# Seven quarter products for the queries and keys of three retention heads, and value groups that add up in PSUM

## The chip, the cores and the metric

The kernel runs on one core of one Trainium2 chip. The metric is device time of one execution in microseconds (us). Engines are named as in the profile: PE is TensorE's matmul row, PEld its weight loads (which overlap PE), DVE is VectorE, ACT is ScalarE, POOL is GpSimd, and SP issues most DMAs.

## The reference, cut to what matters

One transformer block on 512 tokens of width 1024, in float32: a stick-breaking attention with 16 heads and a retention with 4 heads side by side, mixed by gates, then a feed-forward layer. The part that matters here, for each retention head of query/key width 256 and value width 512:

```python
hmix = modulate(rmsnorm(x, g_norm1[l]), shift1, scale1)          # 512 x 1024
proj = jnp.einsum('bsd,de->bse', hmix, w_in[l])
sb_q, sb_k, sb_v, r_q, r_k, r_v, r_g, br = jnp.split(proj, IN_SPLITS, axis=-1)
...
rq = rotary(r_q.reshape(b, s_len, RET_HEADS, RET_QK_DIM))
rk = rotary(r_k.reshape(b, s_len, RET_HEADS, RET_QK_DIM)) * (RET_QK_DIM ** -0.5)
rv = r_v.reshape(b, s_len, RET_HEADS, RET_V_DIM)
o_ret = retention(rq.transpose(0, 2, 1, 3), rk.transpose(0, 2, 1, 3), rv.transpose(0, 2, 1, 3))
o_ret = head_rmsnorm(o_ret.transpose(0, 2, 1, 3)).reshape(b, s_len, RET_V_WIDTH)
o_ret = jax.nn.silu(r_g) * o_ret
... jnp.einsum('bse,ed->bsd', o_ret, w_proj_ret[l]) ...
```

The rotary turn takes the first and second 128 of a head's 256 columns as a pair and gives `t1*cos - t2*sin` and `t1*sin + t2*cos`.

## The kernel before

**Precision.** Every float32 operand of a matmul is split in two: ScalarE copies it, rounded, to a high part (`hi`), and VectorE subtracts to get the low part (`lo`). `mm3` then issues three matmuls, high by high, high by low, low by high. `weight(key)` loads 512 KB of weights into a buffer "raw" (three of them) and splits them (lines 206 and 208); `sv_parts` does the same for weights that are loaded already (lines 879 and 883). The split weights lie in four "whi" and four "wlo" buffers, 128 x 1024 each.

**The seven products.** A product of a 2 x 2 block matrix by another can be done with seven block products in place of eight. The kernel does so for the value and gate columns of retention heads 1 to 3 (the groups "vg") and for the stick-breaking values (group "sv"). The activations' block sums S1 to S4 are formed once (`sv_acts`) and stay in SBUF, keyed A11, A12, A22, S1, S2, S3, S4. For each group, `seven` loads the weights' quarters b11, b12, b21, b22, forms their sums on VectorE (`sub`, line 1006), splits them, and calls `sv_product` once for each key: 24 matmuls of 512 columns into two PSUM banks. The feed-forward part does the same with `product`, 24 matmuls of 256 columns into one bank.

**How a group adds up before the change.** P1 (the product A11) is copied from PSUM to SBUF by ScalarE (line 1028), A12 is added to it in PSUM and stored, and the other sums are formed on VectorE from an SBUF tile and a PSUM bank: P1 + S2 (line 1051), + S3 (1056), + A22 (1061); S1 is copied out (1066) and added (1070), S4 goes on in S1's banks and is added last (1073). The order of products is A11, A12, S2, S3, the scores, A22, S1, the outputs, S4. In the last group ("sv") there are no scores and outputs, and A11 comes ahead of the gate and the projection.

**A retention head.** In the loop over `h` the order on TensorE is: `ret_qk(h + 1)`, the queries and keys of the next head by four `gemm`s of 8 x 3 matmuls of 512 columns, with head `h`'s gate (`ret_gate`, 16 transposes, line 787) in between; then `seven`, which runs the projection of head `h` (`ret_proj`, eight gemms of 12 matmuls over the weights "pr") and the value group of head `h + 1` with its scores and outputs. `ret_gate` needs all four products of VectorE at line 783. The rotary turn (lines 699 to 701, then a split into a "q" tile) reads the queries and keys from PSUM.

**Buffers.** PSUM has eight banks: four "ps", three "z", one "av". The SBUF tags that the change touches are "raw" (3) and "araw" (2) for loaded weights, "s" (8 tiles of 128 x 1024), "t" (7 of 128 x 512) and "q" (8).

**Order.** Outside a few blocks, the order of the instructions on each engine is made when the program is built, by a scheduler that follows the order in which they are written but takes a later one where an earlier one is not ready by its own estimate. Each engine then works through its list in that order. DMAs stand in SP's list in the same way, and a load that waits for its buffer holds up the loads behind it.

Of the kernel before, what the change touches and what calls it, by code (L numbers as in the profile page):

```python
# [19 lines left out]
P = 128  # L20
# [23 lines left out]
def weight_plan():  # L44
# [20 lines left out]
    for h in range(RH):  # L65
        for i in range(2):
            add(("rq", h, i), "w_in", 0, 8, rng(C_RQ + h * RK + i * P, P))
        for i in range(2):
            add(("rk", h, i), "w_in", 0, 8, rng(C_RK + h * RK + i * P, P))
        if h == 0:  # L70
            for part in range(4):
                add(("rg", 0, part), "w_in", part * 256, 2, rng(C_RG, 512))
        for i in range(4):
            add(("pr", h, i), "w_proj_ret", h * RV, 4, rng(i * 256, 256))
# [41 lines left out]
def kernel(  # L116
# [567 lines left out]
    def ret_qk(h, banks=None, between=lambda: None):  # L684
        res = []
        for key in ("rq", "rk"):
            if banks:
                p1, p2 = banks.pop(0), banks.pop(0)
            else:
                p1, p2 = ps(), ps()  # L690
                gemm(p1, weight((key, h, 0)), hs)
                if key == "rq" and h > 1:
                    between()
                gemm(p2, weight((key, h, 1)), hs)
                if key == "rq" and h == 1:
                    between()
            for c1, c2, op in ((cosT, sinT, ALU.subtract), (sinT, cosT, ALU.add)):
                m1, m2 = tmp(), tmp()
                nc.vector.tensor_mul(m1, p1, c1)
                nc.vector.tensor_mul(m2, p2, c2)  # L700
                nc.vector.tensor_tensor(m1, m1, m2, op=op)
                hl = pair("q")
                split(hl[:, 0, :], hl[:, 1, :], m1)
                res.append(hl)
        return res
# [302 lines left out]
    def seven(name, h, gate, store, scores=lambda: None, outs=lambda: None, first=False, early=3):  # L1008
# [14 lines left out]
        p1 = [tmp() for _ in PI]  # L1023

        def opening():
            x = sv_product("A11", w1)
            for t, o in zip(p1, x):
                nc.scalar.activation(t, o, AF.Copy)  # L1028
            return x

        if first:
            ahead(0)
            ahead(1)
            x = opening()
# [5 lines left out]
        if not first:  # L1040
            x = opening()
# [5 lines left out]
        w7 = [sv_parts(t) for t in b12]  # L1047
        for two in loaded:
            ada_after(last_low[0], two)
        for t, o in zip(p1, sv_product("S2", w6)):  # L1050
            nc.vector.tensor_add(t, t, o)
        w4 = [sv_parts(t) for t in b21]
        b22 = [sv_raw(name, 1, 1, n, "s") for n in PI]
        u3 = [tmp() for _ in PI]
        for t, u, o in zip(u3, p1, sv_product("S3", w7)):
            nc.vector.tensor_add(t, u, o)
        w5 = [sv_parts(t) for t in b11]
        scores()
        c21 = [tmp() for _ in PI]
        for t, u, o in zip(c21, u3, sv_product("A22", w4)):  # L1060
            nc.vector.tensor_add(t, u, o)
        store(1, 0, c21)
        x = sv_product("S1", w5)
        c22 = [tmp() for _ in PI]
        for t, o in zip(c22, x):
            nc.scalar.activation(t, o, AF.Copy)
        w3 = [sv_parts(t) for t in b22]
        outs()
        for t, u in zip(c22, u3):
            nc.vector.tensor_add(t, t, u)  # L1070
        store(1, 1, c22)
        for t, o in zip(p1, sv_product("S4", w3, x)):
            nc.vector.tensor_add(t, t, o)
        store(0, 1, p1)

    qk = ret_qk(0, qk_ps)
# [8 lines left out]
    for h in range(3):  # L1085
        ys = []
        qk = ret_qk(h + 1, between=lambda: ys.extend(ret_gate(h, *outs, sgs)))
# [790 lines left out]
```

## Time and profile before

| | |
|---|---|
| Time, median of 3 runs | 1110.66 us (1110.65 to 1110.95) |
| Profiled execution, span | 1109.0 us |
| PE busy | 1101.6 us (99%) |
| PEld busy | 940.5 us (85%) |
| DVE busy | 868.6 us (78%) |
| ACT busy | 564.8 us (51%) |
| POOL busy | 43.3 us (4%) |
| DMA | 181.41 MB, mean 164 GB/s |

The profiled execution has no time of its own beside its span; the runs' median stands 1.7 us above that span. Busy time of PE is modelled, since matmuls overlap: a row's duration is longer than the distance to the next row, and the distance is what counts. A line "L229" is the one line in `mm` that issues all matmuls, so matmuls are told apart by their tiles: "ps<-h,whi" writes a "ps" bank, with the moving operand in an "h" tile and the weights in "whi". In the windows view each engine's busy time in a stretch is followed by the number of instructions in brackets.

### The profile page before, as it was taken

The numbers are of one execution on the slowest core, as the hardware profiler recorded it, in microseconds if no ns is written. First come the engines' busy times: TensorE is split into PE (matmuls) and PEld (weight loads), VectorE is DVE, ScalarE is ACT, GpSimd is POOL, SyncE is SP. The second block draws the span as 40 slices with busy tenths as digits, with TensorE's granted clock in tenths as the row PEclk, the third lists the DMA queues.
The fourth block names the chain that finished last, engine by engine and source line by source line (L and its number), as shares of the span: only waits on it lengthen the run. The fifth ranks groups of instructions, "written<-read, shape, count | busy, mean of one in ns | idle before, by whom it ended". The sixth has DMA issues, their size and how long they took to land.

```text
span 1109.0 us, 15098 instructions
## 1 busy us (share of the span) xinstructions
PE 1101.6 (99%) x5635; PEld 940.5 (85%) x5635; DVE 868.6 (78%) x1292; ACT 564.8 (51%) x935; POOL 43.3 (4%) x69
## 2 busy tenths in 40 slices
PE   9999999999999999999999999999999999999997
PEld 7888888888888888888888888889988888888887
DVE  7996967848868759478678876667999988888875
ACT  5454445445444645265565654357745644554445
POOL 0000000010020020000000000000000000000000
PEclk9999999999999999999999999999999999999999
DMA  8733662583486295887676448662443544444112
GB/s 339 295 108 103 215 206 85 172 208 114 155 177 219 78 206 180 225 237 226 187 200 174 144 159 307 241 171 58 130 138 115 151 133 133 131 117 124 67 39 76
DMA packets 59112, 181.41 MB, mean 164 GB/s; under 512 B 7328, under 2 KB 8352, under 8 KB 59040
## 3 DMA queue, kind: packets, MB, share of 16 engines
q1 hardware_dynamic: 53568, 166.82, 45.9%
q0 software_dynamic: 5472, 13.63, 7.8%
q8 instruction: 44, 0.72, 0.3%
q14 instruction: 28, 0.23, 0.1%
HBM read 148.97 MB, written 16.78 MB: 149 GB/s over the span
## 4 chain that ended last, share of the span: by engine, by line
PE 96%; DVE 2%; ACT 1%; issue 0%; DVEq 0%; ACTq 0%
PE ps L229 71%; PE z L229 14%; PE av L229 8%; PE ps L651 1%; PE z L787 0%; PE av L651 0%; ACT q L1234 0%; DVE h L1544 0%; DVE s L1279 0%; DVE h L1279 0%; DVE o L1214 0%; ACT h L1545 0%; PE av L787 0%; ACT t L1708 0%; DVE h L1608 0%
## 5 line engine op out<-in xcount | busy, mean ns | idle before, releaser
L229 PE MATMUL ps<-h,whi 128*128 128x512 f32 (+1 forms) x1026 | 293.2, 372 | 0.0
L229 PEld LDWEIGHTS ps<-h,whi 128*128 128x128 f32 x1026 | 184.1, 189 | 30.9 <-ACT h L440 0.2
L206 ACT ACTIVATE whi<-raw 128x1024 fp32r<-128x1024 f32 (+1 forms) x104 | 108.7, 1045 | 187.6 <-PE ps L229 142.1
L229 PE MATMUL ps<-h,wlo 128*128 128x512 f32 (+1 forms) x513 | 187.9, 370 | 0.0
L208 DVE TENSOR_TENSOR wlo<-raw,whi 128x1024 fp32r<-128x1024 f32 (+1 forms) x104 | 124.7, 1199 | 57.6 <-ACT whi L206 57.0
L229 PEld LDWEIGHTS ps<-h,wlo 128*128 128x128 f32 x513 | 96.7, 188 | 16.5
L229 PE MATMUL ps<-s,whi 128*128 128x512 f32 x320 | 98.9, 390 | 0.0
L229 PE MATMUL ps<-q,whi 128*128 128x512 f32 (+1 forms) x368 | 98.5, 385 | 0.0
L883 DVE TENSOR_TENSOR wlo<-s,whi 128x1024 fp32r<-128x1024 f32 x46 | 56.1, 1220 | 40.4 <-ACT whi L879 40.4
L229 PEld LDWEIGHTS ps<-q,whi 128*128 128x128 f32 x368 | 67.9, 188 | 13.5 <-DVE t L1372 0.2
L879 ACT ACTIVATE whi<-s 128x1024 fp32r<-128x1024 f32 x47 | 49.7, 1057 | 50.2 <-PE ps L229 44.3
L229 PE MATMUL ps<-whi,h 128*128 128x512 f32 x222 | 71.6, 391 | 0.0
L229 PEld LDWEIGHTS ps<-s,whi 128*128 128x128 f32 x320 | 60.1, 188 | 12.7 <-DVE s L208 0.3
L229 PE MATMUL ps<-s,wlo 128*128 128x512 f32 x160 | 62.3, 389 | 0.0
L229 PE MATMUL ps<-q,wlo 128*128 128x256 f32 (+1 forms) x328 | 59.3, 293 | 0.0
L229 PEld LDWEIGHTS ps<-q,wlo 128*128 128x128 f32 x328 | 48.2, 190 | 3.3
L229 PEld LDWEIGHTS ps<-whi,h 128*128 128x128 f32 x222 | 41.7, 188 | 9.5 <-ACT t L1028 0.6
L229 PE MATMUL ps<-wlo,h 128*128 128x512 f32 x111 | 43.3, 390 | 0.0
L229 PE MATMUL ps<-whi,q 128*128 128x512 f32 x128 | 40.7, 389 | 0.0
L641 DVE TENSOR_TENSOR_SCAN s<-s,table 128x1024 f32<-128x1024 f32 x16 | 36.6, 2288 | 4.6 <-ACT s L635 4.5
L229 PE MATMUL z<-q,q 128*128 128x256 f32 (+3 forms) x224 | 40.1, 325 | 0.0
L229 PEld LDWEIGHTS z<-q,q 128*128 128x128 f32 x224 | 34.8, 189 | 3.0 <-DVE q L208 0.2
(364 smaller groups left out, 2200.0 us busy)
## 6 DMA issues: line engine op xcount, KB each, us to landing
raw<-wp SPq DMA_DIRECT2D x136, 512.0 KB, 3.9
araw<-wp SPq DMA_DIRECT2D x30, 512.0 KB, 4.4
s<-wp SPq DMA_DIRECT2D x24, 512.0 KB, 5.2
s<-wada SPq DMA_DIRECT2D x20, 512.0 KB, 7.4
sraw<-wada SPq DMA_DIRECT2D x16, 512.0 KB, 8.5
q<-qp SPq DMA_DIRECT2D x32, 256.0 KB, 4.3
araw<-wada SPq DMA_DIRECT2D x12, 512.0 KB, 4.6
spill<-o POOLq DMA_DIRECT2D x24, 256.0 KB, 4.7
```

What stands on the lines that cost most here:

```text
L206: nc.scalar.activation(dst_hi, src, AF.Copy, scale=scale)
L208: return (eng or nc.vector).tensor_sub(dst_lo, src, f(dst_hi))
L229: return nc.tensor.matmul(o, lhs, rhs, start=start, stop=stop, skip_group_check=True).ins
L641: nc.vector.tensor_tensor_scan(n[:, ::-1], n[:, ::-1], d[:, ::-1], 0.0, op0=ALU.mult, op1=ALU.max)
L651: nc.tensor.transpose(at[bank][:, c : c + P], t[:, a + j * P : a + (j + 1) * P], ident)
L879: nc.scalar.activation(hi, t, AF.Copy)
L883: last_low[0] = nc.vector.tensor_sub(lo, t, f(hi))
```

## The change

The queries and keys of heads 1 to 3 are made by seven products (`quarter_product`, 24 matmuls of 256 columns) from four weight quarters, loaded under the new keys ("qk", h, half, c). The products add up in three PSUM banks: x (A11, then A12), z (a ScalarE copy of A11, then S2, S3, A22), v (S1, then S4). ScalarE copies the results to SBUF tiles `q` and `k` in the order that the rotary turn wants; two VectorE adds complete the keys. The weight sums are formed on VectorE in the loaded buffers. The gate of the head before (`between`) comes after the second product.

The value groups keep their seven products but add up in the same way: x's two banks are copied by ScalarE to two more banks z, S2, S3 and A22 go on in z, with copies out after S2 and S3, and four VectorE adds remain of ten. Their order is now A11, A12, S2, S1, S3, the scores, A22, the outputs, S4.

```diff
--- before.py
+++ after.py
@@ -63,11 +63,11 @@
         add(("sq", p), "w_in", 0, 8, rng(C_Q + p * P, P))
         add(("sk", p), "w_in", 0, 8, rng(C_K + p * P, P))
     for h in range(RH):
-        for i in range(2):
-            add(("rq", h, i), "w_in", 0, 8, rng(C_RQ + h * RK + i * P, P))
-        for i in range(2):
-            add(("rk", h, i), "w_in", 0, 8, rng(C_RK + h * RK + i * P, P))
-        if h == 0:
+        if h:
+            for half in range(2):
+                for c, at in enumerate((C_RQ, C_RK)):
+                    add(("qk", h, half, c), "w_in", half * 512, 4, rng(at + h * RK, RK))
+        else:
             for part in range(4):
                 add(("rg", 0, part), "w_in", part * 256, 2, rng(C_RG, 512))
         for i in range(4):
@@ -681,27 +681,16 @@
 
     head_pe = {}
 
-    def ret_qk(h, banks=None, between=lambda: None):
+    def rotary(p1, p2):
         res = []
-        for key in ("rq", "rk"):
-            if banks:
-                p1, p2 = banks.pop(0), banks.pop(0)
-            else:
-                p1, p2 = ps(), ps()
-                gemm(p1, weight((key, h, 0)), hs)
-                if key == "rq" and h > 1:
-                    between()
-                gemm(p2, weight((key, h, 1)), hs)
-                if key == "rq" and h == 1:
-                    between()
-            for c1, c2, op in ((cosT, sinT, ALU.subtract), (sinT, cosT, ALU.add)):
-                m1, m2 = tmp(), tmp()
-                nc.vector.tensor_mul(m1, p1, c1)
-                nc.vector.tensor_mul(m2, p2, c2)
-                nc.vector.tensor_tensor(m1, m1, m2, op=op)
-                hl = pair("q")
-                split(hl[:, 0, :], hl[:, 1, :], m1)
-                res.append(hl)
+        for c1, c2, op in ((cosT, sinT, ALU.subtract), (sinT, cosT, ALU.add)):
+            m1, m2 = tmp(), tmp()
+            nc.vector.tensor_mul(m1, p1, c1)
+            nc.vector.tensor_mul(m2, p2, c2)
+            nc.vector.tensor_tensor(m1, m1, m2, op=op)
+            hl = pair("q")
+            split(hl[:, 0, :], hl[:, 1, :], m1)
+            res.append(hl)
         return res
 
     def tok_proj_wide(banks, ws):
@@ -1020,60 +1009,110 @@
             elif i == 3:
                 sub(b12, b11, b11)
 
-        p1 = [tmp() for _ in PI]
-
-        def opening():
-            x = sv_product("A11", w1)
-            for t, o in zip(p1, x):
+        def copied(z, us):
+            for t, o in zip(us, z):
                 nc.scalar.activation(t, o, AF.Copy)
-            return x
+            return us
 
         if first:
             ahead(0)
             ahead(1)
-            x = opening()
+            x = sv_product("A11", w1)
         ys = gate()
         ret_proj(h, ys, ahead)
         b21 = [sv_raw(name, 1, 0, n, "raw") for n in PI]
         sub(b22, b12, b12)
         sub(b22, b11, b22)
         if not first:
-            x = opening()
+            x = sv_product("A11", w1)
+        z = copied(x, [ps() for _ in PI])
         w2 = [sv_parts(r) for r in b21]
         loaded = [ada_early("s") for _ in range(early)]
         w6 = [sv_parts(t) for t in b22]
         sub(b21, b22, b21)
         store(0, 0, sv_product("A12", w2, x))
-        w7 = [sv_parts(t) for t in b12]
+        w5 = [sv_parts(t) for t in b11]
         for two in loaded:
             ada_after(last_low[0], two)
-        for t, o in zip(p1, sv_product("S2", w6)):
+        sv_product("S2", w6, z)
+        u2 = copied(z, [tmp() for _ in PI])
+        w7 = [sv_parts(t) for t in b12]
+        v = sv_product("S1", w5)
+        b22 = [sv_raw(name, 1, 1, n, "s") for n in PI]
+        w4 = [sv_parts(t) for t in b21]
+        sv_product("S3", w7, z)
+        c22 = copied(z, [tmp() for _ in PI])
+        scores()
+        for t, o in zip(c22, v):
             nc.vector.tensor_add(t, t, o)
-        w4 = [sv_parts(t) for t in b21]
-        b22 = [sv_raw(name, 1, 1, n, "s") for n in PI]
-        u3 = [tmp() for _ in PI]
-        for t, u, o in zip(u3, p1, sv_product("S3", w7)):
-            nc.vector.tensor_add(t, u, o)
-        w5 = [sv_parts(t) for t in b11]
-        scores()
-        c21 = [tmp() for _ in PI]
-        for t, u, o in zip(c21, u3, sv_product("A22", w4)):
-            nc.vector.tensor_add(t, u, o)
-        store(1, 0, c21)
-        x = sv_product("S1", w5)
-        c22 = [tmp() for _ in PI]
-        for t, o in zip(c22, x):
-            nc.scalar.activation(t, o, AF.Copy)
+        store(1, 1, c22)
         w3 = [sv_parts(t) for t in b22]
+        store(1, 0, sv_product("A22", w4, z))
         outs()
-        for t, u in zip(c22, u3):
-            nc.vector.tensor_add(t, t, u)
-        store(1, 1, c22)
-        for t, o in zip(p1, sv_product("S4", w3, x)):
+        for t, o in zip(u2, sv_product("S4", w3, v)):
             nc.vector.tensor_add(t, t, o)
-        store(0, 1, p1)
-
-    qk = ret_qk(0, qk_ps)
+        store(0, 1, u2)
+
+    def quarter_product(key, w, o, first=False):
+        hi, lo = (tiles(t) for t in w)
+        ah, al = sacts[key]
+        for i in PI:
+            c, oc = slice(i * P, i * P + P), o[:, i * 256 : i * 256 + 256]
+            for k in range(4):
+                mm3(oc, hi[:, k, c], lo[:, k, c], ah[k], al[k],
+                    first and i == 0 and k == 0, i == 1 and k == 3)
+
+    def ret_qk(h, between):
+
+        def load(half, c, tag):
+            r = wpool.tile([P, WCOLS], F32, tag=tag, bufs=BUFS[tag], name=nm(tag))
+            nc.sync.dma_start(r, wp[WIDX["qk", h, half, c]])
+            return r
+
+        def turned(t):
+            return t.rearrange("p (f h c) -> p h f c", f=2, h=2)
+
+        def as_two(o):
+            return o.rearrange("p (f c) -> p f c", f=2)
+
+        b11, b12 = (load(0, c, "araw") for c in PI)
+        b21, b22 = (load(1, c, "raw") for c in PI)
+        w1 = sv_parts(b11)
+        nc.vector.tensor_sub(b11, b12, b11)
+        w5 = sv_parts(b11)
+        nc.vector.tensor_sub(b12, b22, b12)
+        w3 = sv_parts(b22)
+        nc.vector.tensor_sub(b22, b22, b11)
+        x, z, v = ps(), ps(), ps()
+        quarter_product("A11", w1, x, True)
+        nc.scalar.activation(z, x, AF.Copy)
+        quarter_product("S1", w5, v, True)
+        w6 = sv_parts(b22)
+        between()
+        p5 = tmp()
+        nc.scalar.activation(p5, v, AF.Copy)
+        quarter_product("S2", w6, z)
+        w7 = sv_parts(b12)
+        q, k = raw_quarter("s"), raw_quarter("s")
+        kt, qt = turned(k), turned(q)
+        nc.scalar.activation(kt[:, 0], as_two(z), AF.Copy)
+        quarter_product("S4", w3, v)
+        nc.vector.tensor_add(kt[:, 0], kt[:, 0], as_two(v))
+        w2 = sv_parts(b21)
+        nc.vector.tensor_sub(b21, b21, b22)
+        quarter_product("S3", w7, z)
+        nc.scalar.activation(kt[:, 1], as_two(z), AF.Copy)
+        nc.vector.tensor_add(kt[:, 1], kt[:, 1], as_two(p5))
+        w4 = sv_parts(b21)
+        quarter_product("A12", w2, x)
+        nc.scalar.activation(qt[:, 0], as_two(x), AF.Copy)
+        k1, k2 = rotary(k[:, 0:S], k[:, S:])
+        quarter_product("A22", w4, z)
+        nc.scalar.activation(qt[:, 1], as_two(z), AF.Copy)
+        q1, q2 = rotary(q[:, 0:S], q[:, S:])
+        return q1, q2, k1, k2
+
+    qk = rotary(*qk_ps[:2]) + rotary(*qk_ps[2:])
     vt = ret_v(v_ps)
     st = ret_scores(0, qk)
     sgs = ret_silu(0)
@@ -1084,7 +1123,7 @@
     outs = ret_out(0, st, vt)
     for h in range(3):
         ys = []
-        qk = ret_qk(h + 1, between=lambda: ys.extend(ret_gate(h, *outs, sgs)))
+        qk = ret_qk(h + 1, lambda: ys.extend(ret_gate(h, *outs, sgs)))
         st, outs = {}, []
         vt = lambda: [rvts[b] for b in range(4)]
         seven(("vg", h + 1), h, lambda: ys, rv_store, lambda: st.update(ret_scores(h + 1, qk)),
```

## The prediction

> **What bounds the kernel now.** I read the page first: its busy shares and the chain of work that ended last.
>
> ```profile
> span 1109.0 us, 15098 instructions
> PE 1101.6 (99%) x5635; PEld 940.5 (85%) x5635; DVE 868.6 (78%) x1292; ACT 564.8 (51%) x935; POOL 43.3 (4%) x69
> PEclk9999999999999999999999999999999999999999
> PE 96%; DVE 2%; ACT 1%; issue 0%; DVEq 0%; ACTq 0%
> ```
>
> TensorE is on the chain for 96% of the span at an undiminished clock, so a change pays only as it shortens TensorE's row, or costs as it opens gaps in it. Next the busy times by stretch. The last five of the first six rows below are one retention head (92.8 to 187.0); the seventh row is the next head's queries and keys; the last two rows are a pure 512-column stretch and one of the feed-forward part, whose products already have the new form.
>
> ```profile
> core 0: us, PE busy (x) PEld busy (x) DVE busy (x) ACT busy (x) POOL busy (x), PEclk, DMA share, GB/s
> 86.00:92.80 6.80, 6.80 (x32) 5.63 (x31) 2.79 (x4) 5.26 (x13) 0.00 (x0) 1.00 0.01 5
> 92.80:116.30 23.50, 23.50 (x113) 19.71 (x112) 18.97 (x40) 8.87 (x13) 0.00 (x0) 1.00 0.49 169
> 116.30:138.10 21.80, 21.80 (x98) 18.05 (x97) 19.98 (x21) 9.19 (x14) 0.00 (x0) 1.00 0.58 196
> 138.10:159.90 21.80, 21.80 (x97) 17.86 (x96) 11.88 (x18) 9.08 (x11) 0.00 (x0) 1.00 0.70 234
> 159.90:181.60 21.70, 21.70 (x104) 18.16 (x103) 17.60 (x28) 12.50 (x21) 2.55 (x4) 1.00 0.24 89
> 181.60:187.00 5.40, 5.40 (x26) 4.46 (x25) 4.02 (x16) 1.75 (x3) 0.00 (x0) 1.00 0.01 2
> 187.00:210.50 23.50, 23.50 (x113) 19.72 (x112) 19.29 (x26) 10.48 (x14) 0.00 (x0) 1.00 0.51 181
> ...
> 106.50:159.50 53.00, 53.00 (x236) 1.00 0.62 209
> ...
> 785.00:795.00 10.00, 10.00 (x85) 10.00 (x85) 9.86 (x13) 5.99 (x9) 0.00 (x0) 1.00 0.34 76
> ```
>
> TensorE is busy for the whole of every row: the retention heads have no gap that the change could close. VectorE is second: 18.97 + 19.98 + 11.88 + 17.60 + 4.02 = 72.5 of 94.2 us in the head, fullest just where the change adds to it (116.3 to 138.1: 92%), with some 10 us free behind that. The clock is 1.00 throughout.
>
> **TensorE's saving.** Queries and keys of heads 1 to 3 are now four gemms of 8 x 3 matmuls of 512 columns, 96 a head. They become seven products of 2 x 4 x 3 = 24 matmuls of 256 columns, 168 a head. The prices are in TensorE's timeline: 24 of 512 columns, and 24 of 256 in the same order of hi and lo, each read to the start of the next row.
>
> ```profile
> 138.07 5.60 PE L229 MATMUL ps<-v,h 128*128 128x512 f32 x24
> 143.51 0.39 PE L229 MATMUL ps<-whi,q 128*128 128x512 f32 x1
> ...
> 781.95 3.04 PE L229 MATMUL z<-q,h 128*128 128x256 f32 x24
> 784.83 3.04 PE L229 MATMUL ps<-v,s 128*128 128x256 f32 x24
> ```
>
> (143.51 - 138.07) / 24 = 0.2267 us and (784.83 - 781.95) / 24 = 0.120 us. So 96 x 0.2267 = 21.76 becomes 168 x 0.120 = 20.16: 1.60 us a head, 4.80 us for three. An eighth of the columns goes, but a 256-column matmul costs 6.7 ns more than half a 512-column one, which takes 1.1 of the 2.7 us. The weight-load column says why: 10.00 of 10.00 us at 785 against about 18 of 21.8 in the 512-column rows, so there the loads set the pace.
>
> [...]
>
> **New waits on PSUM.** The value groups keep x (two banks) and now copy it by ScalarE to z (two more of the four "ps" banks); A12 goes on in x; S2, S3 and A22 add into z in turn. Before, S2 had fresh banks and one of its matmuls slipped in (143.51) while the copies ran. Now S2 needs the copy too and S1 finds no bank, so A12's first matmul waits. The old last group shows that wait uncovered: S1 ends, its banks are copied (L1066), S4 goes on in them.
>
> ```profile
> 431.15 1.28 ACT L1066 ACTIVATE t<-ps 128x512 f32<-128x512 f32 x2 [0.93 <-PE ps L229]
> 431.18 0.39 PE L229 MATMUL ps<-wlo,q 128*128 128x512 f32 x1
> 431.41 0.39 PE L229 MATMUL ps<-whi,q 128*128 128x512 f32 x1
> ...
> 431.81 0.50 PE L229 MATMUL ps<-whi,o 128*128 128x512 f32 x1
> ```
>
> 431.81 - 431.41 - 0.227 = 0.17 us. It comes three times (A11 to A12; in the last group x is ready a whole projection earlier) and once in the last group from S3 to A22, which in the heads has the scores between; the old S1-to-S4 wait goes. Net 3 x 0.17 = 0.51 us. Bounds: 0 (filled, as at 143.51) to 4 x 1.28 = 5.1 (both copies bare); I take the row of the same wait. The other reuses have a product or the scores between: S2 to S3 has S1, S1 to S4 has A22 and the outputs. S1 still takes x's banks only after the store of A12, as S3 did. A22 now directly precedes the outputs (S1 stood there): their first nine matmuls need only the older value blocks, 9 x 0.227 = 2.0 us against one 0.6 split and one 0.68 subtraction, and S4 can be put in; 0.
>
> **VectorE and ScalarE.** The prices, from the groups by line (VectorE's counted from 60 to 440 us, ScalarE's over the whole run):
>
> ```profile
> L883 DVE TENSOR_TENSOR wlo<-raw,whi 128x1024 fp32r<-128x1024 f32 x16 | 19.3, 1220 | 10.2 <-ACT whi L879 10.2
> L208 DVE TENSOR_TENSOR q<-t,q 128x512 fp32r<-128x512 f32 x16 | 10.9, 682 | 0.4 <-ACT q L206 0.4
> L1006 DVE TENSOR_TENSOR s<-s,s 128x1024 f32<-128x1024 f32 x8 | 9.5, 1216 | 0.0
> L1051 DVE TENSOR_TENSOR t<-t,ps 128x512 f32<-128x512 f32 x8 | 5.4, 680 | 0.0
> L1070 DVE TENSOR_TENSOR t<-t,t 128x512 f32<-128x512 f32 x8 | 5.3, 688 | 0.3 <-ACT t L1066 0.3
> ...
> L879 ACT ACTIVATE whi<-raw 128x1024 fp32r<-128x1024 f32 x19 | 20.2, 1061 | 29.6 <-PE ps L229 26.7 <-DVE mod L265 1.6 <-PE av L229 1.3
> ...
> L1028 ACT ACTIVATE t<-ps 128x512 f32<-128x512 f32 x8 | 4.8, 598 | 11.7 <-PE ps L229 11.4
> ```
>
> Each head's queries and keys gain three low parts and four weight sums (7 x 1.22 = 8.5) and two adds (1.4): +9.9 us of VectorE. Each value group loses six of its ten adds (L1051, L1056, L1061, L1070, L1073, two each): 6 x 0.68 = -4.1. Net +5.8 us a head: 78.3 of 92.8 us, 84%; on the whole it fits. ScalarE gains three high parts (3.2), six copies (3.6) and two in the group (1.2): +8 us on 41 of the head's 94; hidden.
>
> Where it is tight is the queries' and keys' stretch, 20.2 + 2.0 (transposes) = 22.2 us from A11's start (t = 0). The four whi/wlo buffers let the low parts for A11 and S1 be made behind the old A22, during the outputs and S4, where VectorE is least loaded. From t = 0: last adds 1.4, S4's part, the sum, S2's part 3.7, four gate parts 2.7, S3's part 1.2, adds and sums 2.6, parts for A12 and A22 2.4: 14 us for 22.2, before any rotation. Buffer by buffer: S2's part is made by about 4 and needed at 7.8; S3's by 6, at 13.5; A12's by 9, at 16.4; A22's by 13, at 19.3. Leads of 4 to 7 us. The rotations (16 x 0.68 = 10.9) move behind, into the projection's first 10 us, and push the group's weight sums into the idle third behind 138. In the 785 stretch VectorE is 9.86 of 10 us busy and TensorE has no gap. Bounds for late weights: 0, to what rival B gives; I allow 0.17 us, the shortest wait shown, for each product group of a head: 0.51.
>
> **Queues.** A head's four loads stay 512 KB each on SP's queue; two move from "raw" to "araw" buffers. SP's later loads queue behind them: in head 1 the two modulation loads wait for the second "araw" release at about t = 6; in the later value loads b22 waits for the "s" buffers of the unrotated q and k, free at about t = 30, needed by t = 44.
>
> ```profile
> raw<-wp SPq DMA_DIRECT2D x136, 512.0 KB, 3.9
> araw<-wp SPq DMA_DIRECT2D x30, 512.0 KB, 4.4
> ```
>
> At 4 us a load both are hidden; if not, 4.4 us once. POOL's queue is untouched. The gate's transposes come 5.8 us into the stretch (10.9 before in head 1, 5.4 in 2 and 3). Head 1's four gate products then end just in time, head 2's earlier:
>
> ```profile
> 98.34 0.74 DVE L783 SCALAR_TENSOR_TENSOR t<-av,sm,t 128x512 f32<-128x512 f32 x1
> ...
> 189.92 1.40 DVE L783 SCALAR_TENSOR_TENSOR t<-z,sm,t 128x512 f32<-128x512 f32 x2
> ```
>
> Head 1: 98.34 + 0.74 = 99.1 against 92.8 + 5.8 = 98.6; 0.5 us late, covered by S2, whose weights are ready from the idle 86 to 92.8. Head 2: 4.3 us behind the start at 187.0; in time.
>
> **Sum.** -4.80 + 0.51 + 0.51 = -3.78 us on the profiled span of 1109.0: 1105.2. The median of the runs, 1110.66, stands 1.7 above that span; I keep that difference: **1106.9 us**. A difference under 0.2% (2.2 us: 1108.4 to 1112.9) counts as no change.
>
> **Rivals.** *B, slower: the projection's first weights stand behind the rotation.* Both are VectorE's, and the rotation is written earlier. If q's rotation (8 x 0.68 = 5.4, beginning a copy of 0.6 after A22) is served first, TensorE waits 0.6 + 5.4 + 1.2 = 7.2 us in each head; half of it in front gives 3.6, so -3.8 + 10.8: **1117.7**. It cancels the gain from 1.3 us a head and is slower from 2.0. For: VectorE is 92% busy in that stretch. Against: the weights' input is ready seven us before q is, and today the two kinds alternate without a gap. *C, no change: bank reuse in the quarter products.* Five reuses a head (A11-S2, S2-S3, S1-S4, A11-A12, S3-A22); at 0.17 each 15 x 0.17 = 2.6: **1109.5**. Against: a product of 2.9 us stands between, and copy and add take 1.3. *D, slower: the last group's z is taken while the last projection runs.* x already holds two of the four banks; with one left each of eight gemms shows its copy, 8 x (0.59 + 0.17) = 6.1: **1113.0**. For: x is complete long before; against: z's copies are written behind the projection. *E: the 256-column matmul runs at half the 512-column price,* 0.1133: 2.7 us a head, 1103.5 after the same waits. [...]
>
> **How the numbers follow.** Forecast 0.64, with its own range 1105.0 to 1108.4 (no wait at all gives 1110.7 - 4.8 = 1105.9; another 0.9 is a quarter of the way from there to E); B 0.12, C 0.17, D 0.05, E 0.02. Faster 0.66, same 0.17, slower 0.17. The range 1105.0 to 1112.0 takes in the forecast and C and leaves out B, D and E, 0.19.
>
> **What would show it.** TensorE's row: seven runs of 24 256-column matmuls per head, 2.88 us each; head to head 1.4 us shorter; a pitch of about 0.4 us once at A12. VectorE nearly full from A11 to the end of the projection, idle time behind it shrunk. Wrong would make it: gaps of over 1 us before S2, A22 or the first projection matmul (B), or a projection of the last head longer than 22 us (D).

## The result, and the profile after

The changed kernel takes **1112.22 us** (median; 1111.07 to 1114.87), the kernel before 1110.66 us (1110.25 to 1111.1) beside it: a ratio of 1.0018, interval 1.0011 to 1.0024. The forecast was 1106.9 us in a range of 1105.0 to 1112.0, and faster. The kernel is 1.6 us slower instead. Its 17 runs also spread four times as far, 3.8 us against 0.9.

The page of the profile after: span, busy times, chain of work that ended last.

```profile
span 1110.2 us, 15580 instructions
PE 1098.1 (99%) x5851; PEld 945.5 (85%) x5851; DVE 882.8 (80%) x1295; ACT 585.4 (53%) x970; POOL 40.8 (4%) x69
PE 88%; DVE 7%; ACT 2%; DMA 1%; issue 1%; SPq 0%; DVEq 0%; ACTq 0%
```

TensorE is busy for 3.5 us less, and the span is 1.2 us longer. Its share of the chain fell from 96 to 88%, VectorE's rose from 2 to 7%: TensorE now waits for VectorE. Where, says the waits view of the changed kernel for TensorE's matmuls, 88 to 500 us (who waited for whom: total us, times, longest; for the kernel before, this view is empty for that stretch):

```profile
PE ps L229 <- DVE wlo L208: 1.5, 1, 1.5
PE z L776 <- DVE t L772: 1.3, 1, 1.3
PE ps L229 <- DVE s L208: 0.6, 1, 0.6
PE ps L229 <- DVE wlo L872: 0.5, 1, 0.5
```

A stretch is named here after the head whose queries and keys open it; the gate and the projection in it work on the outputs of the head before. The first wait is in head 1's projection (from 127.7 us: 1.69 us between two matmuls beyond the usual distance), the second at the first transpose of head 1's gate (95.0: 1.50), the third at the last projection, in the last group (382.9: 0.81), the fourth at S3 of head 1's value group (163.3: 0.70). From head to head (the starts of A11's first matmul at 92.26, 189.12, 282.20 and 375.27, the last of them the last group's, and the first stick-breaking turn at 483.41) the lengths are 96.86, 93.08, 93.07 and 108.14 us, against 94.21, 94.08, 94.09 and 107.03 before: +2.65, -1.00, -1.02, +1.11. So the gain is there in heads 2 and 3, and head 1 and the last group take back more than it.

Busy time by stretch after: queries and keys and projection of head 1, the same of head 2, and head 3's projection; then head 3's projection before.

```profile
92.30:115.70 23.40, 22.06 (x185) 21.86 (x184) 20.26 (x39) 11.43 (x17) 0.00 (x0) 1.00 0.41 139
115.70:139.30 23.60, 22.08 (x98) 17.95 (x97) 22.33 (x27) 12.33 (x18) 0.00 (x0) 1.00 0.77 255
...
189.10:211.00 21.90, 21.90 (x185) 21.88 (x184) 18.97 (x24) 13.26 (x19) 0.00 (x0) 1.00 0.41 128
211.00:233.20 22.20, 22.12 (x98) 17.96 (x97) 22.20 (x26) 12.33 (x19) 6.12 (x7) 1.00 0.96 231
...
304.10:326.30 22.20, 22.09 (x99) 17.95 (x98) 22.20 (x26) 12.25 (x19) 5.97 (x7) 1.00 0.98 234
```

```profile
304.60:326.40 21.80, 21.80 (x98) 18.05 (x97) 16.94 (x18) 9.19 (x14) 5.96 (x7) 1.00 0.75 144
```

The last two rows are the ones that matter. During head 3's projection VectorE was busy for 16.94 of 21.80 us before and is busy for 22.20 of 22.20 us after; the DMA engines went from 0.75 to 0.98. In head 1's projection VectorE has 22.33 of 23.60. That TensorE waits where VectorE's list puts something else in front of what it needs is what the experiments below test.

The saving itself, from TensorE's timeline of head 2: the starts of A11's and S1's first two matmuls.

```profile
189.12 0.40 PE L229 MATMUL ps<-h,whi 128*128 128x256 f32 x2
...
191.99 0.40 PE L229 MATMUL ps<-q,whi 128*128 128x256 f32 x2
```

(191.99 - 189.12) / 24 = 0.1196 us a matmul, as forecast.

### The profile page after: what moved, and what is told of

Read it like the earlier page. It is cut to its first block, busy times and chain, and to the rows that moved or that the text cites. A ratio compares the mean times of both kernels' runs of the same rounds, so it can differ in the third digit from the quotient of the medians.

```text
span 1110.2 us, 15580 instructions
## 1 busy us (share of the span) xinstructions
PE 1098.1 (99%) x5851; PEld 945.5 (85%) x5851; DVE 882.8 (80%) x1295; ACT 585.4 (53%) x970; POOL 40.8 (4%) x69
## 2 busy tenths in 40 slices
DMA packets 59115, 181.45 MB, mean 163 GB/s; under 512 B 7328, under 2 KB 8352, under 8 KB 59040
## 4 chain that ended last, share of the span: by engine, by line
PE 88%; DVE 7%; ACT 2%; DMA 1%; issue 1%; SPq 0%; DVEq 0%; ACTq 0%
PE ps L229 64%; PE z L229 14%; PE av L229 8%; PE ps L651 1%; DVE wlo L208 1%; DVE t L690 1%; DVE wlo L872 1%; DVE t L689 1%; DVE s L262 1%; DMA x<-xT 0%; DMA raw<-wp 0%; DVE t L688 0%; ACT whi L206 0%; DVE q L208 0%; ACT whi L868 0%
## 5 line engine op out<-in xcount | busy, mean ns | idle before, releaser
L229 PE MATMUL ps<-h,whi 128*128 128x512 f32 (+1 forms) x978 | 260.0, 355 | 0.0
L229 PEld LDWEIGHTS ps<-h,whi 128*128 128x128 f32 x978 | 170.9, 189 | 23.8 <-ACT h L440 0.2
L206 ACT ACTIVATE whi<-raw 128x1024 fp32r<-128x1024 f32 (+1 forms) x92 | 95.8, 1041 | 168.4 <-PE ps L229 137.7
L229 PE MATMUL ps<-h,wlo 128*128 128x512 f32 (+1 forms) x489 | 170.9, 353 | 0.0
L208 DVE TENSOR_TENSOR wlo<-raw,whi 128x1024 fp32r<-128x1024 f32 (+1 forms) x92 | 110.1, 1197 | 63.9 <-ACT whi L206 63.4
L229 PE MATMUL ps<-q,whi 128*128 128x512 f32 (+1 forms) x464 | 116.3, 365 | 0.0
L229 PEld LDWEIGHTS ps<-q,whi 128*128 128x128 f32 x464 | 83.0, 189 | 13.3
L229 PE MATMUL ps<-q,wlo 128*128 128x256 f32 (+1 forms) x376 | 72.9, 292 | 0.0
L868 ACT ACTIVATE whi<-raw 128x1024 fp32r<-128x1024 f32 x31 | 32.9, 1061 | 47.5 <-PE ps L229 28.6
L872 DVE TENSOR_TENSOR wlo<-raw,whi 128x1024 fp32r<-128x1024 f32 x29 | 35.2, 1221 | 14.4 <-ACT whi L868 14.4
```

What stands on the lines that cost most here:

```text
L206: nc.scalar.activation(dst_hi, src, AF.Copy, scale=scale)
L208: return (eng or nc.vector).tensor_sub(dst_lo, src, f(dst_hi))
L229: return nc.tensor.matmul(o, lhs, rhs, start=start, stop=stop, skip_group_check=True).ins
L868: nc.scalar.activation(hi, t, AF.Copy)
L872: last_low[0] = nc.vector.tensor_sub(lo, t, f(hi))
```

## The experiments

All kernels were timed in five rounds beside the kernel before, whose median was 1110.43 to 1110.52 us in the four series. Line numbers shift between kernels: the split of a projection weight is L206 (high part, ScalarE) and L208 (low part, VectorE) in the changed kernel and L210 and L212 in some others; `sv_parts` has its high part at L866 to L873 and its low part at L870 to L877, in "groups alone" at L883 as before.

### Which half of the change costs: groups alone, queries and keys alone

```diff
 # groups alone: ret_qk and the weight plan as before, seven() as changed
 # queries and keys alone: ret_qk as changed, seven() as before
```

> Only the value groups are changed; queries and keys of heads 1 to 3 stay four gemms. Theory 1 (the loss sits in places: head 1, and the last group): heads 1 to 3 pay about 0.1 to 0.2 us each at A12 and the last group about 1.1 us, so 1.3 to 1.7 us over the kernel before, 1112.1. Theory 2 (VectorE is too full everywhere, and the groups relieve it by 4 us each): no slower than before, 1110.2 to 1110.7.

> Only the queries and keys of heads 1 to 3 are changed; the value groups add up as before. Theory 1: 4.8 us saved on TensorE, head 1 gives back about 3.9 (gate 1.5, projection weights 1.7, S3 weights 0.7), the projections of heads 2 and 3 0.4 each: 1110.5, and the last group costs nothing. Theory 2: VectorE carries 9.9 us more a head with no relief, so heads 2 and 3 lose their gain too: 1114 or more.

Groups alone: 1112.67 us (ratio 1.002, 1.0011 to 1.0029). Queries and keys alone: 1110.05 (0.9999, 0.9991 to 1.0008). Theory 1 comes nearer in both, though the groups cost 0.5 us more than it allows; theory 2 fails in both. The effects add up: +2.2 and -0.4 us, against +1.6 to 1.7 for the whole change. TensorE's waits of the two, groups first:

```profile
PE ps L229 <- DVE s L208: 0.6, 1, 0.6
PE ps L229 <- DVE wlo L883: 0.5, 1, 0.5
```

```profile
PE ps L229 <- DVE wlo L208: 2.1, 1, 2.1
PE z L776 <- DVE t L772: 1.3, 1, 1.3
```

The four waits of the changed kernel fall apart into two and two. The waits at S3 and in the last projection belong to the value groups, the gate and head 1's projection to the quarter products. With the old groups heads 2 and 3 are 1.1 us shorter each, and head 1 is 2.4 us longer.

### Head 1's gate as a whole behind S4

```diff
-        between()                       # after S1
+        if h > 1: between()
...
+        if h == 1:
+            with tc.issue_after(held):  # last matmul of S4
+                between()
```

> The changed kernel, with head 1's gate after the fourth quarter product (S4) instead of the second, and held there on TensorE. Theory 1: the 1.5 us wait of the first transpose goes, and nothing takes its place: 1110.7. Theory 2: VectorE still has the same work in the same stretch, the wait moves to the next weights: 1112.2 as the changed kernel.

1114.02 us (1.0036, 1.0023 to 1.0048), above both. The wait at the transpose is gone, but head 1 is as long as before the edit (91.47 against 91.42 us, counted here and below from the end of one head's output matmuls to the end of the next head's). TensorE now waits for VectorE's splits of q at the scores, which the list has put inside the projection (0.88 and 0.28 us idle), and for a split of ScalarE at an output matmul inside S3 (1.17). A wait removed was not time gained; the gate wait is not the last limit of head 1. The other 1.8 us of the median are not explained by head 1.

### Head 1 as before, heads 2 and 3 by quarter products

```diff
+        if h == 1:
+            return ret_qk1(between)     # four gemms of 512 columns
```

> The changed kernel, with head 1's queries and keys by four gemms again (gate between them, as before). Theory 1: head 1 costs what it cost before (94.2 us instead of 96.9), heads 2 and 3 keep their 1.0 us each, the last group its loss of 1.1: 1112.2 - 2.6 = 1109.6, faster than the kernel before by 0.1%. Theory 2: a third of the change is undone and the loss shrinks by a third: 1111.7.

1111.03 us (1.0003, 0.9995 to 1.0012), nearer to theory 2, which gives no reason. The profile does: theory 1 left out that head 1 still pays 0.70 us at S3, beside the 1.1 us of the last group. The same with the old groups:

> The value groups of the kernel before everywhere, quarter products for heads 2 and 3 alone, head 1 by the four products of the kernel before. If the parts add up: head 1 88.8 us and heads 2 and 3 some 93.0 us each in place of 94.1, so 1110.5 - 2.2 = 1108.3 us, faster than both kernels. Rival: the quarter products of head 2 need what head 1's quarter products set up (the order of the loads), and the loss of head 1 appears in head 2: 1110 us or more.

1108.55 us (0.9984, 0.9975 to 0.9992), as the parts add up: heads 2 and 3 take 92.95 and 92.93 us in place of 94.08 and 94.09.

### The loads or VectorE's list?

In the changed kernel the third projection weight of head 1 looked like a late transfer. ScalarE's timeline, and then VectorE's, of the changed kernel (a bracket gives the idle time before and what ended it):

```profile
117.84 1.06 ACT L206 ACTIVATE whi<-raw 128x1024 fp32r<-128x1024 f32 x1 [2.60 <-DMA raw<-wp]
118.80 0.61 ACT L206 ACTIVATE q<-t 128x512 fp32r<-128x512 f32 x1
```

```profile
119.45 0.69 DVE L208 TENSOR_TENSOR q<-t,q 128x512 fp32r<-128x512 f32 x1 [1.27 <-ACT q L206]
...
125.51 2.35 DVE L872 TENSOR_TENSOR v<-s,v 128x1024 fp32r<-128x1024 f32 x2
127.78 0.68 DVE L208 TENSOR_TENSOR q<-t,q 128x512 fp32r<-128x512 f32 x1
128.38 1.22 DVE L208 TENSOR_TENSOR wlo<-raw,whi 128x1024 fp32r<-128x1024 f32 x1
```

The third weight's high part waits 2.60 us for its load, the rotation's split stands behind it, and VectorE idles for 1.27 us. But this high part is made by 118.90, and the low part, which TensorE needs, follows only at 128.38: it also stands behind two low parts of the *next* group's first weights ("v<-s", 2.35 us). Three kernels were built to tell loads from list. The "pair" in them is two loads and two products of 1.22 us on VectorE (L262) for a later part of the block, which stand behind head 1's gate before and after the change:

```diff
 # early sum: A22's weight sum goes to the idle tile of A11's weights, so that raw b22 comes free a gate earlier
+        nc.vector.tensor_sub(b11, b21, b22)
         between()
...
-        nc.vector.tensor_sub(b21, b21, b22)
 # without the pair: the two modulation products leave head 1's gate for a later place
-        for _ in range(1 if h == 0 else 0):
-            ada_after(ins)
```

> Changed kernel, but A22's weight sum (A21 minus A22) is written into the idle tile of A11's weights right behind S2's parts, so that A22's raw tile comes free one gate earlier and the projection's second and third weight can be loaded then. Theory 1 (late transfers: the projections wait because their raw tiles are held until that sum): the wait of 1.69 us in head 1's projection goes and the projections of heads 2 and 3 fall from 22.20 to 21.76 us each, 1112.2 - 1.7 - 0.9 = 1109.6 us. Theory 2 (VectorE is simply full there, whatever is loaded when): projections as they are, 1112.2 us, within 0.4.

> Changed kernel, but the two modulation loads and their two 1.22 us products that stand behind head 1's gate are left to a later place (the FFN's). Theory 1 (late transfers): VectorE reaches A22's weight sum 2.4 us earlier, the loads of the projection's weights follow, the 1.69 us wait goes and the 0.70 us at S3 of the value group, which comes from other products, stays: 1112.2 - 1.7 = 1110.5 us. Theory 2 (VectorE full): 2.4 us less of its work take 2.4 us of the 3.9 us of head 1's waits, in whichever stand last: 1109.8 us. Theory 3 (the waits come from the order of the queues, not from the load): the wait moves to another place of head 1, 1112.2 us.

> Both edits together. Theory 1: head 1's projection as in heads 2 and 3 (from 23.6 to some 21.8 us), those of heads 2 and 3 at 21.76 us; the gate's 1.50 and the 0.70 us at S3 stay: 1112.2 - 1.8 - 0.9 = 1109.5 us. Theory 2: no more than without the early sum, 1109.8 to 1110.5 us, heads 2 and 3 at 93.07 us.

Early sum: 1116.87 us (1.0055, 1.0042 to 1.0067), a miss for both theories, and no clean test in head 1: the tile of A11's weights is now held until A22's parts are made, so the two modulation loads share the other tile of that kind and come at 102.21 and 107.95 in place of 93.00 and 102.09. The pair's products then wait 2.7 us on VectorE for them, with all that stands behind them in its list. The loads of the projection's second and third weight do come earlier (99.10 and 109.09 against 109.92 and 112.33), yet the third's low part starts at 129.72, later than the 128.38 above, and TensorE waits 3.26 us for it. Without the pair: 1111.29 (1.0009, 1.0000 to 1.0018). Both: 1111.95 (1.0013, 1.0004 to 1.0022); heads 2 and 3, where the early sum stands alone, keep projections of 22.2 us. Counted from the start of head 2's projection, the loads of its second and third weight come 6.4 and 3.7 us earlier with both edits than without the pair alone, and the third's low part starts 10.37 us behind that start in both kernels. Earlier loads gained nothing, so theory 1 falls as far as heads 2 and 3 go. The trace shows why: without the pair the third weight has landed at 208.54, its high part is made by 211.60, and its low part starts at 220.05, with VectorE busy all the while. Without the pair head 1's projection shrinks from 23.63 to 22.20 us, like the others, and the 1.50 and 0.70 us stay; the medians show 0.9 us of these 1.4, between theory 1 and theory 3, and in the profile head 2 is 0.3 us longer.

### The gate's transposes, then the order on VectorE

```diff
 # hold: without the pair, and head 1's 16 transposes behind S2
+                if gate_behind:
+                    held.enter_context(tc.issue_after(gate_behind[0]))
 # first parts later: A11's parts of a group ahead of the fourth projection weight, not the second
-            elif i == 1 and not w1:
-                w1.extend(sv_parts(r, False, ...) for r in b11)
...
             elif i == 3:
+                if not first:
+                    w1.extend(sv_parts(r, False, "vv") for r in b11)
```

> Changed kernel without the modulation pair behind head 1's gate (as in the kernel before this one, 1111.3 us), and head 1's 16 transposes are held behind the product S2; VectorE's gate work stays where it was. Theory 1 (TensorE's list: one transpose stands right behind A11, 4.4 us before VectorE's chain of 13 small operations and four products allows it): the 1.50 us goes, head 1's queries and keys and gate fall from 23.4 to some 22.0 us, 1111.3 - 1.4 = 1109.9 us. Theory 2 (the gate's work itself is late, wherever the transposes stand): the splits behind them come 1.3 us later and the projection's first weights with them, 1111.3 us.

> Quarter products for heads 2 and 3 alone, groups of the kernel before (1108.6 us), and the parts of the value group's first weights are made one projection weight later. Theory 1 (order on VectorE: the third projection weight's low part stands behind those parts, 2.35 us): the projections of heads 2 and 3 fall from 22.2 to 21.8 us, 1108.6 - 0.9 = 1107.7 us. Theory 2 (VectorE full between the last product and the third weight, with both rotations there): the wait moves to the fourth weight or to A11, 1108.6 us.

Hold: 1111.28 us, no change against 1111.29. VectorE's low part of the third weight of head 1's projection, without the pair and with hold:

```profile
126.17 1.22 DVE L208 TENSOR_TENSOR wlo<-raw,whi 128x1024 fp32r<-128x1024 f32 x1
```

```profile
126.23 1.23 DVE L208 TENSOR_TENSOR wlo<-raw,whi 128x1024 fp32r<-128x1024 f32 x1
```

TensorE is ahead by 1.3 us and meets the same low part within 0.1 us of the same moment: its wait at the transpose shrinks from 1.50 to 0.18 us and the one in the projection grows from 0.28 to 1.35. This is why removing the gate wait did not pay. Behind both stands VectorE's list.

First parts later, on heads 2 and 3 with the old groups: 1107.07 us (0.997, 0.9959 to 0.9982) against 1108.55. Theory 1 gives 0.9 us of these 1.5, and the profiles show them (0.5 in head 2, 0.5 in head 3); another 0.5 us of the profiles' difference lies ahead of 86 us, where the two kernels are alike. The third weight in head 2's projection without the edit, its high part on ScalarE first, and then with the edit:

```profile
209.75 1.05 ACT L210 ACTIVATE whi<-raw 128x1024 fp32r<-128x1024 f32 x1
...
216.38 2.35 DVE L876 TENSOR_TENSOR v<-s,v 128x1024 fp32r<-128x1024 f32 x2
218.65 0.68 DVE L212 TENSOR_TENSOR q<-t,q 128x512 fp32r<-128x512 f32 x1
219.25 1.22 DVE L212 TENSOR_TENSOR wlo<-raw,whi 128x1024 fp32r<-128x1024 f32 x1
```

```profile
215.84 1.23 DVE L212 TENSOR_TENSOR wlo<-raw,whi 128x1024 fp32r<-128x1024 f32 x1
216.98 0.69 DVE L212 TENSOR_TENSOR q<-t,q 128x512 fp32r<-128x512 f32 x1
217.58 2.36 DVE L876 TENSOR_TENSOR v<-s,v 128x1024 fp32r<-128x1024 f32 x2
```

Without the edit the high part is there by 210.80 and the low part starts at 219.25, so it is VectorE that the weight waits for. Counted from the end of head 1's outputs (181.55 and 181.02) the low part is made 2.9 us earlier, and the projection is 21.79 us in place of 22.22. Nothing was taken off VectorE; only the order changed.

### The value groups' two waits

```diff
 # S3's parts ahead of the modulation products; the last group as before
         w5 = [sv_parts(t) for t in b11]
+        w7 = [sv_parts(t) for t in b12]
         for two in loaded:
             ada_after(last_low[0], two)
...
-    seven("sv", 3, ...)
+    seven_old("sv", 3, ...)
```

> Changed kernel with two edits of the value groups at places 200 us apart: the parts of S3's weights (w7) are written ahead of the six modulation products instead of behind them (as in the kernel before), and the last group is built as in the kernel before. Theory (order of the lists): the 0.70 us at S3 in head 1 goes, and the last group falls by 1.1 us, from 108.1 to 107.0: 1112.2 - 1.8 = 1110.4 us, with the 1.50 and 1.69 us in head 1 as they were. Rival for S3 (VectorE has 7.3 us of modulation products too many there): the wait moves to S1 or A22, 1111.1 us.

1110.62 us (1.0006, 0.9997 to 1.0015), the first theory's 1110.4 within 0.2. The S3 wait is gone and the last group takes 112.45 us in place of 113.58, counted from the end of head 3's outputs. How its wait arose, on ScalarE and VectorE before, and then after:

```profile
380.19 1.28 ACT L1028 ACTIVATE t<-ps 128x512 f32<-128x512 f32 x2 [1.04 <-PE ps L229]
381.99 1.89 DVE L208 TENSOR_TENSOR s<-z,s 128x512 fp32r<-128x512 f32 x3 [0.23 <-ACT s L206]
```

```profile
380.97 1.06 ACT L206 ACTIVATE whi<-raw 128x1024 fp32r<-128x1024 f32 x1 [1.71 <-PE ps L229]
382.06 1.23 DVE L208 TENSOR_TENSOR wlo<-raw,whi 128x1024 fp32r<-128x1024 f32 x1 [0.19 <-ACT whi L206]
383.20 1.88 DVE L208 TENSOR_TENSOR s<-z,s 128x512 fp32r<-128x512 f32 x3
```

Before, ScalarE's two copies of P1 (L1028, 1.28 us) stood between the weights' splits and the gate's; without them a projection weight that isn't needed yet goes ahead of the gate's splits, which TensorE is waiting for, and they come 1.21 us later on the two clocks, 1.11 counted from A11's first matmul. This is read from the two lists; the experiment put back the last group as a whole.

The profiled execution of this kernel is its longest, 1113.75 us, and had a wait that the other profiles lack there: ScalarE's v<-s stood for its load in head 3's projection.

```profile
ACT v L868 <- DMA s<-wp: 2.3, 1, 2.3
317.20:320.60 3.40, 3.40 (x8) 2.64 (x9) 3.40 (x4) 0.00 (x0) 0.14 (x1) 0.53 1.06 163
```

ScalarE's later splits stood behind it, and TensorE waited 2.27 us for the third weight in place of 0.28. The second line is the windows view just behind that wait: the granted clock is 0.53, and matmuls of 512 columns start every 0.427 us in place of 0.227, which costs another 1.6 us (3.40 x 0.200 / 0.427). So head 3's projection took 25.78 us in place of 22.20. A late load like this was seen in one profile.

### All edits together, and what each is worth

> Quarter products for heads 1 to 3, groups of the kernel before, no modulation pair behind head 1's gate, head 1's transposes behind S2, the group's first parts one projection weight later. If every wait named above is mended: three heads at 1.6 us less each, 1110.5 - 4.8 = 1105.7 us. If the mended order opens waits elsewhere in head 1: no better than heads 2 and 3 alone, 1107.7 us.

> The changed kernel with all edits of order: no modulation pair behind head 1's gate, transposes behind S2, the group's first parts one projection weight later, S3's parts ahead of the modulation products, and the last group built as in the kernel before. It differs from the best kernel so far (1106.1 us) only in how the three heads' value groups add up. Theory 1 (the new sums cost the short waits between A11 and A12, as the prediction had it): 3 x 0.1 to 0.17 us more, 1106.4 to 1106.6 us. Theory 2 (the groups' other order of parts and products costs more): 1107.5 us or above.

> The best kernel so far with the modulation pair back behind head 1's gate. Theory 1 (VectorE's list is full from head 1's gate to the third projection weight, and the loads of the projection's weights wait for it): its two products of 1.22 us come back as a wait in the projection, 1106.1 + 1.5 to 2.4 = 1107.6 to 1108.5 us. Theory 2 (with the group's first parts later there is room): 1106.1 us.

> The best kernel so far with head 1's transposes where the scheduler puts them. Theory 1: the wait of 1.50 us at the transpose is back and is now paid, 1106.1 + 1.3 = 1107.4 us. Theory 2 (TensorE arrives at the third projection weight before VectorE has made it in any case, so that a wait ahead of it costs nothing): 1106.1 us.

| kernel | us | ratio to before |
|---|---|---|
| best: quarter products in heads 1 to 3, old groups, no pair, transposes behind S2, first parts later | 1106.06 | 0.9963 (0.9950 to 0.9975) |
| mended: the same, with the changed value groups in the heads, S3's parts early | 1107.12 | 0.9969 (0.9956 to 0.9981) |
| best with the pair back | 1108.17 | 0.9982 (0.9973 to 0.9991) |
| best with the transposes where the scheduler puts them | 1108.49 | 0.9985 (0.9976 to 0.9994) |

Best is faster than both kernels. Its heads take 87.44, 92.60 and 92.52 us, against 88.77, 94.08 and 94.09 before; TensorE's waits view is empty again between 90 and 490 us. Behind that a wait is new: 0.90 us at 716.80, in the feed-forward part, for a VectorE split of an h tile. Mended and best with free transposes have it too (0.73 and 1.12 us), the kernels before and after and best with the pair back do not. Its cause was not followed up: the pair now stands in that part, but "without the pair" moves it there too and has no such wait. So the heads are 4.4 us shorter and the span only 3.3. The page of best:

```profile
span 1105.7 us, 15614 instructions
PE 1097.6 (99%) x5851; PEld 947.1 (86%) x5851; DVE 896.2 (81%) x1319; ACT 583.9 (53%) x962; POOL 43.4 (4%) x69
PE 95%; DVE 2%; ACT 2%; DMA 0%; issue 0%; DVEq 0%; ACTq 0%
```

VectorE is busy for 13.4 us more than in the changed kernel, and the kernel is 6 us faster: the sum of VectorE's work was not what cost the time.

With the third weight in time, the transposes' place is worth 2.4 us by the medians, where it was worth nothing in "hold". The heads of the profiles show 1.3 of it, in head 1, where the gate's wait is back; the rest is not explained. The pair back costs 2.1 us by the medians, as theory 1 has it. The waits of its profile in head 1, TensorE's and then ScalarE's:

```profile
PE ps L229 <- ACT whi L206: 2.3, 2, 2.0
PE ps L229 <- DVE wlo L877: 0.4, 1, 0.4
```

```profile
ACT whi L206 <- DMA raw<-wp: 3.6, 2, 2.0
```

This execution took 1110.88 us, 2.7 more than the median, and only one of the other ten took as long, so its waits are not what the usual 2.1 us consist of. In it the loads do come too late: the pair's products delay the weight sum L1124 that frees a raw tile (the second weight's load at 110.30, for which ScalarE waits 1.6 us), and the load of the third projection weight, at 115.59, stands on SP's queue behind a load of the next group that waits 3.5 us for its buffer; it lands 2.0 us after ScalarE is ready for it. Behind TensorE's wait of 2.0 us the clock is again 0.51, from 124.30 to 127.80. What the pair costs in the usual execution was not profiled.

Mended's heads take 87.48, 92.64 and 92.64 us in the profile, within 0.12 us of best, and its interval overlaps best's: the changed sums in PSUM cost little or nothing beside the old ones in the heads. Whether the 1.1 us between the medians is real stays open.

## Why the prediction was wrong, point by point

**TensorE's saving** was right: 0.1196 us a matmul against 0.120, 1.6 us a head, and PE's chain is back at 95% once the waits are gone. That the weight loads set this pace was the author's reading of their busy share (10.00 of 10.00 us before, and 15.80 of 15.80 in the changed kernel's quarter products from 189.2 to 205.0); TensorE's matmul row is as full in both stretches, and no run tells the two apart.

**New waits on PSUM** were right in size. S3 to A22 in the last group: 427.58 - 427.18 - 0.227 = 0.17 us, the forecast's number; A11 to A12 in the heads: one score matmul slips in and 0.1 us is left. Wrong was that the last group has no such wait because x is ready a projection earlier: the copies of x are written behind the projection (the second is made at 406.92 to 407.50), and A12 waits 0.26 us there.

```profile
407.18 0.87 PE L229 MATMUL ps<-whi,h 128*128 128x512 f32 x2
407.89 0.39 PE L229 MATMUL ps<-wlo,h 128*128 128x512 f32 x1
...
427.18 0.39 PE L229 MATMUL ps<-whi,qp 128*128 128x512 f32 x1
427.58 0.50 PE L229 MATMUL ps<-whi,h 128*128 128x512 f32 x1
```

(407.89 - 407.18 - 2 x 0.227 = 0.26.)

**VectorE's work** was right as a sum: 882.8 - 868.6 = +14.2 us, forecast 3 x 5.8 - 4.1 = 13.3. **Its place is the step that failed.** "The rotations move behind, into the projection's first 10 us, and push the group's weight sums into the idle third" supposed that the projection's own weights go ahead of both. They do not: the first low part goes ahead of the rotation and the second stands among its products, but the rest of its 10.9 us and the next group's first parts fill VectorE's list up to the third. The walk through the stretch also left out the pair's 2.4 us behind head 1's gate. The term "late weights", 0.17 us a head, measured 0.44 us in heads 2 and 3 and 1.87 in head 1 (projections of 22.20 and 23.63 us against 21.76).

**The gate of head 1** was to be "0.5 us late, covered by S2". It stood 1.50 us bare: the scheduler put one transpose in front of S1 (the other fifteen ahead of S2). TensorE's matmuls ran in that order: the transpose started at 96.64, S1's first matmul followed at 96.72, and no product behind the transpose covered its wait. The same shows on ScalarE in that projection: the split of q at 118.80, whose input VectorE had made by 116.44, stands behind a high part that waits 2.60 us for its load.

```profile
95.01 0.28 PE L229 MATMUL ps<-h,wlo 128*128 128x256 f32 x1
96.64 0.33 PE L776 MATMUL z<-con,t 128*128 128x128 f32 x1 [1.34 <-DVE t L772]
96.72 0.48 PE L229 MATMUL ps<-q,whi 128*128 128x256 f32 x2
```

**Queues.** "At 4 us a load both are hidden" priced the change's own loads at 4 us and did not ask which loads stand behind the raw tiles that the change holds longer. In head 1 the load of the projection's second weight waits for the sum L1102, which stands behind the modulation pair, and the third's for the low part behind that sum (until 112.30).

**The last group** lost 1.1 us. 0.3 of it is A12's wait above; the other 0.8 (0.64 in the projection, 22.80 against 22.16 us, and 0.18 at the transposes ahead of it) came from a removal that was costed as a pure gain: ScalarE's two copies had kept a less urgent split behind the gate's. **S3 in head 1** lost 0.70 us when its parts were moved behind six modulation products (7.3 us of VectorE); the prediction did not list this move. Heads 2 and 3 have the same move and no such wait; why was not followed up.

**Rivals.** B named the right resource and the wrong weight: the third, not the first, and 0.44 us where 3.6 were priced. C's bank reuses did not show. D's sign, a last projection over 22 us, was no sign: it was 22.16 us before the change already, and the 22.80 came from another cause than z's banks. E is refuted by the 0.1196 us.

The terms account for the miss. From 92 us to the first stick-breaking turn the forecast was -3.78 us and the profiles show +1.74, 5.5 apart: 1.50 at the gate, 2.2 more for late weights than the 0.51 allowed, 0.70 at S3 and 1.1 in the last group, less 0.2 at A12, together 5.3.

The forecast of 1106.9 us is about what the kernel takes once the order is mended (1107.12). That is in part luck: mended also moves the pair and keeps the old sums in the last group, and it has the new wait in the feed-forward part. What it shows is that TensorE's saving was there to be had, and that the order kept it back.

## What to carry to other kernels

When work moves on an engine that is off the critical path, walk its list up to the next thing that the bounding engine needs, instruction by instruction; the sum over a stage and each buffer's lead time say nothing on what stands in front. A wait that disappears pays only up to the next wait behind it, so take away both: holding the transposes was worth nothing until the third weight was early. Before a profile is used to explain a median, look whether the profiled execution is a usual one. A removed instruction reorders its neighbours too; look at what moves up into its place.

## What the runs showed of the hardware that was not expected

Three waits of TensorE cost more than their length. In three profiled executions waits of 2.11 ("groups"), 3.26 (early sum) and 2.01 us (best with the pair back) were followed by 3.4 to 5.1 us in which the granted clock was 0.50 to 0.53 and matmuls of 512 columns started every 0.427 us. Behind a wait of 1.52 us in the changed kernel and one of 2.09 us with queries and keys alone the clock stayed at 1.00, so waits of about 2 us came with the low clock (2.01, 2.11) and without it (2.09). The cause was not found.

The DMA engines' busy share of head 3's projection rose from 0.75 to 0.98 (144 to 234 GB/s) with the same bytes over the whole run (181.45 against 181.41 MB). It belongs to the quarter products: the groups alone leave it at 0.77. Which loads moved there was not followed up. The wide spread of the changed kernel's runs, 3.8 us, is not explained either: first parts later has a spread of 0.8 us in seven runs, but best with free transposes, with the same order of the weights, one of 4.1 us in eleven.
